# A hybrid trunk kernel on one core: kept weights reloaded in eight pieces, first write-backs postponed, and GLA score levels computed on half of the partitions

## The chip, the core and the metric

The kernel runs on one core of a Trainium2 chip. A core has a matrix engine (PE, with its weight loads shown as PEld), a vector engine (DVE), a scalar engine (ACT), GpSimd (POOL) and a sync engine (SP) whose instructions here only issue transfers; 16 DMA engines carry them. The metric is the device time of one execution in microseconds (us), lower is better.

## The reference

One layer of a trunk over 2048 tokens of width 1024. A single input projection feeds four groups of heads, each a causal recurrence, and one output projection merges them.

```python
u = rmsnorm(h, norm_w[l])
proj = (u @ w_in[l]).astype(f32)
...
y_a = gla_branch(a_q, a_k, a_v, a_gr, a_z, ...)
y_b = mlstm_branch(...)
y_c = hgrn2_branch(...)
y_d = ssd_branch(d_x, d_B, d_C, d_dt, d_z, ...)
mixed = jnp.concatenate([y_a, y_b, y_c, y_d], axis=-1)
h = h + mixed @ w_out[l]
```

GLA (gated linear attention, 4 heads with keys of width 64) scores a query i against each earlier key j of its chunk of 64 tokens with a decay of its own in each key dimension d:

```python
scores = jnp.einsum('bhid,bhjd,bhijd->bhij', qb, kb, decay)
out = (jnp.einsum('bhij,bhje->bhie', scores, vb)
       + jnp.einsum('bhid,bhde->bhie', qb * jnp.exp(G), state))
```

SSD (Mamba-2) works on chunks of 128 tokens: scores of C against B, masked by decays, applied to the inputs, plus a carried state.

## The kernel before, in words

**Halves and units.** The sequence is worked in two halves of 1024 tokens. In each, ten units follow each other: two of GLA (g0, g1, each a pair of heads, the first head's keys on partitions 0 to 63, the second's on 64 to 127), two of SSD (q0, q1), four of HGRN2 and two pairs of mLSTM. The output projection ends the program.

**Projections.** A unit takes its columns of the input projection in groups of 256 columns (`gqk0` holds queries and keys of g0, `gv0` values and gates, `gz0` the gating path, then g1's; for SSD `sx`, `sbc`, `sz`); there are 30 groups. In the first half a group's raw float32 weights of 1 MB are loaded (`raw`), ACT casts them to a coarse part `hi` (four casts, line 248), DVE computes the remainder `lo` (line 250), and a closure `keep` (line 236) writes both to DRAM as `wk`, called while a later group is loaded. In the second half hi and lo are loaded back from there (line 222). `hi` and `lo` have two buffers each, `raw` one. `weights(key)` hands out a group and starts the load of the next. With activations split the same way into uh and ul, each product is three matmuls (hi·uh, hi·ul, lo·uh) for each of 8 slices k of the 1024 inputs: `ps_c` (channels by 512 tokens), `ps_t` (128 tokens by 256 columns), and `ps_g` (128 tokens by 288, for `gv0`). All of them are issued on line 123, in `mm`.

**The start.** Rows of x (`o_f`, `o_qp`, ... `<-x`, line 169) are squared and summed on ACT (line 173), DVE turns the sums into a scale for each token (`ss`, lines 176 to 180), PE transposes it (`ps_rb`, line 188), and ACT scales the four waiting `ps_g` tiles with it into `o_v` (line 676).

**GLA scores.** `lin_unit` with `nh=2` goes through levels of block width b = 1, 2, 4, 8, 16, 32. At each, DVE multiplies decays into kb (line 516) and qf (line 517), PE multiplies keys by queries into `ps_s`, and DVE copies the entries that belong to the level into the score tiles `ST` under a mask (line 479 for b = 1, 4, 8, 16; lines 561 and 562 for b = 2). For b = 1, 4, 8, 16 a tile `qz` (shown as t2k) is built in which each head's queries stand on that head's partitions with zeros on the other's: POOL clears (line 491), ACT copies (line 492). There are four GLA units in all, so 16 such levels. An fp32 matmul appears as two instructions on PE.

**SSD.** A unit computes the conv inputs, then goes through 8 chunks. A step transposes with `ps_xt` (line 898), computes `ps_s` from `ct` (line 749), DVE forms the masked scores (line 911, from decays loaded as `ab<-rows`, line 884), and PE goes on with `ps_o` and `ps_u`. Between a step's `ps_s` and its `ps_o` stand projection matmuls of other units. Finished outputs go to DRAM as 64 KB stores `y<-t2k` (line 645).

**Order.** A scheduler fixes each engine's order of instructions at build time; an instruction waits for those ahead of it on its engine. All transfers named here are issued from SP in that order and use eight completion counters in turn, so each one waits for the one eight before it.

Of the kernel before, what the change touches and what calls it, by code (L numbers as in the profile page):

```python
# [10 lines left out]
F32 = mybir.dt.float32  # L11
# [10 lines left out]
P = 128  # L22
S = 2048
D = 1024
KT = D // P
TH = 1024
NH = S // TH
C = 128
NC = TH // C
# [87 lines left out]
class Kernel:  # L117
# [91 lines left out]
    def load_w(self, key, cuts=None):  # L209

        nc = self.nc
        gates = key == ("gv", 0)
        n = WG + (NG if gates else 0)
        hi = self.wp.tile([P, KT * (WG + NG)], F32R, tag="hi", name="hi", bufs=2)[:, :KT * n].rearrange("p (k n) -> p k n", k=KT)
        lo = self.wp.tile([P, KT * (WG + NG)], F32R, tag="lo", name="lo", bufs=2)[:, :KT * n].rearrange("p (k n) -> p k n", k=KT)
        self.wready[key] = hi, lo
        if self.ahead_of(key) > 0:
            for k in self.unwritten:
                k()
            self.unwritten = []  # L220
            for t, d in zip((hi, lo), self.wkept[key]):
                nc.sync.dma_start(t.bitcast(F32), d.bitcast(F32))
            return
        raw = self.wp.tile([P, KT * (WG + NG)], F32, tag="raw", name="raw")[:, :KT * n].rearrange("p (k n) -> p k n", k=KT)
        self.wkept[key] = [self.dram.tile([P, KT, n], F32R, tag=f"wk{GIDX[key]}{i}", name="wk") for i in range(2)]

        def part(k0, k1):
            nc.sync.dma_start(raw[:, k0:k1, :WG], self.a["w"][GIDX[key], :, k0:k1])
            if gates:
                nc.sync.dma_start(raw[:, k0:k1, WG:], self.a["wg"][:, k0:k1])  # L230
            nc.scalar.copy(hi[:, k0:k1], raw[:, k0:k1])
            nc.vector.tensor_tensor(lo[:, k0:k1], raw[:, k0:k1], hi[:, k0:k1].bitcast(F32), op=ALU.subtract)

        def keep():
            for d, t in zip(self.wkept[key], (hi, lo)):
                nc.sync.dma_start(d.bitcast(F32), t.bitcast(F32))


        kept, self.unwritten = self.unwritten, [keep]
        if cuts:  # L240
            return [(k0, lambda k0=k0, k1=k1: part(k0, k1)) for k0, k1 in zip(cuts, cuts[1:] + [KT])]
        nc.sync.dma_start(raw[:, :, :WG], self.a["w"][GIDX[key]])
        if gates:
            nc.sync.dma_start(raw[:, :, WG:], self.a["wg"])
        for k in kept:
            k()
        for k0, k1 in ((0, 2), (2, 4), (4, 6), (6, 8)):
            nc.scalar.copy(hi[:, k0:k1], raw[:, k0:k1])  # L248
        for k0, k1 in ((0, 4), (4, 8)):
            nc.vector.tensor_tensor(lo[:, k0:k1], raw[:, k0:k1], hi[:, k0:k1].bitcast(F32), op=ALU.subtract)  # L250
# [186 lines left out]
    def lin_unit(self, nh, f, kb, qp, v, sz, car, eps, ycol, vt=None):  # L437

        nc = self.nc
        rw = P // nh  # L440
        rows = [slice(h * rw, (h + 1) * rw) for h in range(nh)]
# [3 lines left out]
        STs = [self.next_st() for _ in range(nh)]  # L445
# [8 lines left out]
        def mixed(b, q):  # L454

            n = 64 // b
            mx = self.t2k().rearrange("p (c n two b) -> p c n two b", c=NC // 2, two=2, b=b)
            nc.scalar.copy(mx[:, :, :, 0], kb.rearrange("p (c u n two b) -> p c u n two b", c=NC // 2, u=2, two=2, b=b)[:, :, 0, :, 0])
            nc.scalar.copy(mx[:, :, :, 1], flipped(C - 1 - b, 2 * b, n, b))
            ps = self.psp.tile([P, NC // 2, 2, n, b], F32, tag="t", name="ps_s")  # L460
            for c in range(NC // 2):
                self.mm(ps[:, c], mx[:, c].rearrange("p n two b -> p (n two b)"), q[:, 2 * c:2 * c + 2])
            return ps
# [6 lines left out]
        def level(b, q, mo):  # L470

            m = mask[:, mo:mo + 64].rearrange("p (n b) -> p n b", b=b)[:, None]

            def place(h, c0, n, ps):
                if mo == 0:
                    o = STs[h][:, c0:c0 + n].rearrange("p c (n two b) -> p c n b two", two=2, b=1)[:, :, :, :, 0]
                else:
                    o = STs[h][:, c0:c0 + n].rearrange("p c (n two b) -> p c n two b", two=2, b=b)[:, :, :, 1]
                nc.vector.copy_predicated(o, m.to_broadcast([P, n, 64 // b, b]), ps)

            if nh == 1:
                ps = mixed(b, q)
                for t in range(2):
                    o = STs[0][:, t::2].rearrange("p c (n two b) -> p c n two b", two=2, b=b)[:, :, :, int(mo != 0)]
                    m = mask[:, 384 * t + mo:384 * t + mo + 64].rearrange("p (n b) -> p n b", b=b)[:, None]
                    nc.vector.copy_predicated(o, m.to_broadcast([P, NC // 2, 64 // b, b]), ps[:, :, t])
                return
            for g in range(2):
                qz = self.t2k().rearrange("p (c h n b) -> p c h n b", c=4, h=2, b=b)
                for h in range(2):  # L490
                    nc.gpsimd.memset(qz[rows[h], :, 1 - h], 0.0)
                    nc.scalar.copy(qz[rows[h], :, h], q[rows[h], 4 * g:4 * g + 4])
                ps = self.psp.tile([P, 4, 2, 64 // b, b], F32, tag="t", name="ps_s")
                for c in range(4):
                    cc = 4 * g + c
                    self.mm(ps[:, c].rearrange("p h n b -> p (h n b)"), kb[:, cc * C:(cc + 1) * C], qz[:, c].rearrange("p h n b -> p (h n b)"))
                for h in range(2):
                    place(h, 4 * g, 4, ps[:, :, h])

        level(1, qp[:, :, 0].unsqueeze(3), 0)  # L500
        if nh == 1:

# [7 lines left out]
        b = 1  # L510
        while b < C:
            n = TH // (2 * b)
# [14 lines left out]
            if b in (4, 8, 16):  # L527
                level(b, qf.rearrange("p (c n two b) -> p c n two b", c=NC, two=2, b=b)[:, :, :, 1], {4: 192, 8: 256, 16: 320}[b])
                continue
            if nh == 1:  # L530
                ST = STs[0]
                if b == 2:
                    kr = flip_odd()
                    for t in range(2):
                        ps = self.psp.tile([P, 4, 2, 64], F32, tag="t", name="ps_s")
                        for c in range(4):
                            cc = 2 * c + t
                            self.mm(ps[:, c].rearrange("p a b -> p (a b)"), kr[:, c] if t else kb[:, cc * C:(cc + 1) * C], qp[:, cc, 1:3].rearrange("p a b -> p (a b)"))
                        m = mask[:, 384 * t:384 * t + 384]
# [6 lines left out]
                ps = mixed(b, qf.rearrange("p (c n two b) -> p c n two b", c=NC, two=2, b=b)[:, :, :, 1])  # L546
# [5 lines left out]
            if b == 2:  # L552
                for g in range(2):
                    pss = [self.psp.tile([P, 4, 2, 64], F32, tag="t", name="ps_s") for _ in range(nh)]
                    for c in range(4):
                        cc = 4 * g + c
# [9 lines left out]
            elif b == 32:  # L566
                for r, ST in zip(rows, STs):
                    ps = self.psp.tile([P, NC, 32], F32, tag="t", name="ps_s")
# [5 lines left out]
            else:  # L574
                pss = [self.psp.tile([P, NC, 64], F32, tag="t", name="ps_s") for _ in range(nh)]
# [8 lines left out]
        for g in range(2):  # L584
            pt = self.psp.tile([P, 4, P], F32, tag="t", name="ps_kt")
            for c in range(4):
                cc = 4 * g + c
# [17 lines left out]
            for c in range(4):  # L605
                cc = 4 * g + c
# [563 lines left out]
```

## Time and profile before

| | before |
|---|---|
| median of 3 runs | 2164.32 us (2163.56 to 2164.61) |
| profiled execution | 2164.58 us, of which the span in the trace is 2162.8 us |
| mean granted PE clock | 0.988 of full |
| instructions | 34846 |

The span runs from the first to the last recorded instruction; what lies around it is 1.78 us. PE is the engine that is busy nearly all of the time, so the places where it is not are what to look for, and the chain of work that ended last says how long each link of it was.

### The profile page before, as it was taken

What the parts mean: (1) busy time and instruction counts of PE and PEld (TensorE: products, weight loads), DVE (VectorE), ACT (ScalarE), POOL (GpSimd) and SP (SyncE); (2) the same over time, 40 slices, a digit from 0 to 9 for tenths busy, and PEclk for the clock granted to TensorE, in tenths of its full rate; (3) what the DMA queues carried; (4) which work ended last, traced back from release to release, by engine and by line L of the source; (5) the groups of instructions that cost most, each with busy time, mean ns of one, the idle gap of its engine ahead of it and who ended that gap; (6) DMA issues with size and microseconds to landing.
All of it is one profiled execution on the core that took longest, in us unless ns stands there. A gap on an engine that the chain in (4) does not pass through costs nothing.

```text
span 2162.8 us, 34846 instructions
## 1 busy us (share of the span) xinstructions
PE 2101.6 (97%) x13758; PEld 1876.2 (87%) x13758; DVE 1211.3 (56%) x2892; ACT 773.0 (36%) x1947; POOL 81.7 (4%) x160
## 2 busy tenths in 40 slices
PE   7999999999999999999998999999999999999998
PEld 6988889998899999897987888898899998888887
DVE  4564868756676545626374956555654456533332
ACT  6632333444444344444221324333333334212111
POOL 0000011100000000000000111000000000000000
PEclk9999999999999999999998989999999999999999
DMA  8434344444244354521422233222232326422321
GB/s 309 151 109 128 92 152 137 147 138 128 78 121 147 127 176 152 164 101 45 134 62 95 82 104 109 72 68 90 77 119 69 127 90 194 142 97 89 107 73 49
DMA packets 197171, 251.41 MB, mean 116 GB/s; under 512 B 142344, under 2 KB 153720, under 8 KB 178064
## 3 DMA queue, kind: packets, MB, share of 16 engines
q1 hardware_dynamic: 190528, 229.79, 33.6%
q10 hardware_dynamic: 6480, 19.40, 2.6%
q8 instruction: 108, 1.77, 0.3%
q14 instruction: 55, 0.45, 0.1%
HBM read 160.70 MB, written 88.45 MB: 115 GB/s over the span
## 4 chain that ended last, share of the span: by engine, by line
PE 87%; DVE 5%; ACT 4%; DMA 3%; issue 1%; SPq 1%; POOL 0%; ACTq 0%; DVEq 0%
PE ps_t L123 31%; PE ps_c L123 24%; PE ps_out L123 15%; PE ps_o L123 6%; PE ps_s L123 5%; PE ps_u L123 3%; PE ps_g L123 2%; DMA ST<-w_out 1%; DMA t2k<-xT 1%; DVE kb L516 1%; DMA raw<-w 1%; PE ps_xt L898 1%; DVE ST L561 0%; ACT t2k L624 0%; DMA o_f<-x 0%
## 5 line engine op out<-in xcount | busy, mean ns | idle before, releaser
L123 PE MATMUL ps_t<-hi,uh 128*128 128x256 f32 x1920 | 545.0, 284 | 0.5 <-DVE craw L742 0.4
L123 PE MATMUL ps_t<-lo,uh 128*128 128x256 f32 x1920 | 545.5, 284 | 0.0
L123 PE MATMUL ps_t<-hi,ul 128*128 128x256 f32 x1920 | 545.4, 284 | 0.0
L123 PEld LDWEIGHTS ps_t<-hi,uh 128*128 128x128 f32 x1920 | 368.7, 192 | 2.3 <-DVE craw L742 1.0
L123 PEld LDWEIGHTS ps_t<-lo,uh 128*128 128x128 f32 x1920 | 369.2, 192 | 0.8
L123 PEld LDWEIGHTS ps_t<-hi,ul 128*128 128x128 f32 x1920 | 369.0, 192 | 0.5 <-issue 0.4
L123 PE MATMUL ps_c<-uh,hi 128*128 128x512 f32 x896 | 357.8, 400 | 7.3 <-ACT uh L155 7.3
L123 PE MATMUL ps_c<-ul,hi 128*128 128x512 f32 x896 | 355.9, 397 | 0.1
L123 PE MATMUL ps_c<-uh,lo 128*128 128x512 f32 x896 | 355.6, 397 | 0.0
L123 PEld LDWEIGHTS ps_c<-uh,hi 128*128 128x128 f32 x896 | 169.8, 190 | 40.1 <-ACT uh L155 7.7
L123 PEld LDWEIGHTS ps_c<-ul,hi 128*128 128x128 f32 x896 | 169.8, 189 | 33.8 <-DVE ul L156 1.0
L123 PEld LDWEIGHTS ps_c<-uh,lo 128*128 128x128 f32 x896 | 169.8, 190 | 33.5
L301 ACT ACTIVATE v<-ps_t,ss 128x128 f32<-128x128 f32 x128 | 40.3, 362 | 168.0 <-PE ps_t L123 167.9
L980 DVE TENSOR_TENSOR o_sz<-o_sz,ps_out 128x512 f32<-128x512 f32 (+1 forms) x33 | 22.1, 671 | 129.9 <-PE ps_out L123 127.6
L123 PE MATMUL ps_out<-woh,o_qp 128*128 128x512 f32 x288 | 94.2, 395 | 0.0
L296 ACT ACTIVATE sz<-ps_t,ss 128x128 f32<-128x128 f32 (+1 forms) x160 | 54.2, 387 | 102.4 <-PE ps_t L123 95.2
L297 DVE SCALAR_TENSOR_TENSOR sz<-sz,ps_t 128x256 f32<-128x256 f32 (+1 forms) x80 | 37.8, 473 | 80.0 <-ACT sz L296 79.7
L250 DVE TENSOR_TENSOR lo<-raw,hi 128x1024 fp32r<-128x1024 f32 (+1 forms) x58 | 70.7, 1227 | 16.6 <-ACT hi L248 16.2
L248 ACT CAST hi<-raw 128x512 fp32r<-128x512 f32 (+1 forms) x116 | 66.1, 626 | 30.5 <-PE ps_c L123 21.2
L123 PE MATMUL ps_out<-woh,o_v 128*128 128x512 f32 (+1 forms) x213 | 75.4, 389 | 0.0
L784 DVE TENSOR_TENSOR t2k<-t2k,ps_s 128x512 f32<-128x512 f32 x16 | 11.0, 688 | 103.2 <-PE ps_s L123 99.1
L123 PEld LDWEIGHTS ps_out<-woh,o_qp 128*128 128x128 f32 x288 | 54.1, 188 | 12.9
(362 smaller groups left out, 3620.3 us busy)
## 6 DMA issues: line engine op xcount, KB each, us to landing
raw<-w SPq DMA_DIRECT2D x29, 1024.0 KB, 6.7
wk<-hi SPq DMA_DIRECT2D x29, 1024.0 KB, 8.2
wk<-lo SPq DMA_DIRECT2D x29, 1024.0 KB, 9.7
lo<-wk SPq DMA_DIRECT2D x29, 1024.0 KB, 6.8
hi<-wk SPq DMA_DIRECT2D x29, 1024.0 KB, 6.0
y<-t2k SPq DMA_DIRECT2D x256, 64.0 KB, 2.0
t2k<-y SPq DMA_DIRECT2D x64, 256.0 KB, 3.7
t2k<-xT SPq DMA_DIRECT2D x32, 256.0 KB, 4.3
```

The lines of the kernel that those rows point to most:

```text
L123: self.nc.tensor.matmul(out, l, r, start=start, stop=stop, skip_group_check=shared)
L248: nc.scalar.copy(hi[:, k0:k1], raw[:, k0:k1])
L250: nc.vector.tensor_tensor(lo[:, k0:k1], raw[:, k0:k1], hi[:, k0:k1].bitcast(F32), op=ALU.subtract)
L296: nc.scalar.activation(out[:, j], ps[:, j], AF.Tanh, scale=self.rsh[:, t + j:t + j + 1])
L297: nc.vector.scalar_tensor_tensor(out=out, in0=out, scalar=1.0, in1=ps, op0=ALU.add, op1=ALU.mult)
L301: self.nc.scalar.activation(out[:, j], ps[:, j], AF.Identity, scale=sc[:, t + j:t + j + 1])
L516: nc.vector.tensor_tensor(kv[:, :, 0], kv[:, :, 0], pv[:, :, 1:2].to_broadcast([P, n, b]), op=ALU.mult)
L784: nc.vector.tensor_tensor(dt, dt, ps, op=ALU.mult)
L898: nc.tensor.transpose(pt[:, i * P:(i + 1) * P], src[:, cs], self.ident)
L980: nc.vector.tensor_tensor(xt[:, ns], xt[:, ns], ps, op=ALU.add)
```

## The change

Three edits are made at once. In `load_w`, the second half's reload of a group is issued as eight transfers (four pairs of slices k, hi and lo of each in turn, 256 KB each, 288 KB for `gv0`) where there were two of 1 MB. Also in `load_w`, the first write-backs come later: nothing is written at the second group, only the first group's parts at the third, and both the second's and the third's at the fourth; from there on each group's are written at the next, as before. The third group's casts go into the first group's buffer. In `lin_unit` with two heads, the levels b = 1, 4, 8, 16 no longer build `qz`: keys and queries of one head are multiplied on that head's 64 partitions, 16 matmuls of 64 partitions by 64 columns for 8 of 128 by 128, with no clearing and no copies, into one tile for each head, and one masked copy for each head takes the place of two.

```diff
@@ load_w, the second half's reload
-            for t, d in zip((hi, lo), self.wkept[key]):
-                nc.sync.dma_start(t.bitcast(F32), d.bitcast(F32))
+            for k in range(0, KT, 2):
+                for t, d in zip((hi, lo), self.wkept[key]):
+                    nc.sync.dma_start(t[:, k:k + 2].bitcast(F32), d[:, k:k + 2].bitcast(F32))
             return
...
-        kept, self.unwritten = self.unwritten, [keep]
+        n = len(self.wkept)
+        kept = self.unwritten[:1] if n == 3 else [] if n == 2 else self.unwritten
+        self.unwritten = self.unwritten[len(kept):] + [keep]
...
@@ lin_unit, level
-            for g in range(2):
-                qz = self.t2k().rearrange("p (c h n b) -> p c h n b", c=4, h=2, b=b)
-                for h in range(2):
-                    nc.gpsimd.memset(qz[rows[h], :, 1 - h], 0.0)
-                    nc.scalar.copy(qz[rows[h], :, h], q[rows[h], 4 * g:4 * g + 4])
-                ps = self.psp.tile([P, 4, 2, 64 // b, b], F32, tag="t", name="ps_s")
-                for c in range(4):
-                    cc = 4 * g + c
-                    self.mm(ps[:, c].rearrange("p h n b -> p (h n b)"), kb[:, cc * C:(cc + 1) * C], qz[:, c].rearrange("p h n b -> p (h n b)"))
-                for h in range(2):
-                    place(h, 4 * g, 4, ps[:, :, h])
+            pss = [self.psp.tile([P, NC, 64 // b, b], F32, tag="t", name="ps_s") for _ in range(nh)]
+            for c in range(NC):
+                for r, ps in zip(rows, pss):
+                    self.mm(ps[:, c], kb[r, c * C:(c + 1) * C], q[r, c])
+            for ST, ps in zip(STs, pss):
...
+                nc.vector.copy_predicated(o, m.to_broadcast([P, NC, 64 // b, b]), ps)
```

The new order of the engines shows the edits at four engines and in places where the code was not touched.

**The start, SP.** SP's queue right behind the load of `gv0`'s raw weights, before; `wk<-hi` of 128x2048 is the first group's write-back.

```order
L236 DMA wk<-hi 128x2048
L236 DMA wk<-lo 128x2048
L169 DMA o_f<-x 128x1024 x2
L169 DMA o_qp<-x 128x1024
L169 DMA o_kb<-x 128x1024
L169 DMA o_f<-x 128x1024 x2
L169 DMA o_qf<-x 128x1024
L169 DMA o_pl<-x 128x1024
L242 DMA raw<-w 128x2048
```

The same place in the changed kernel:

```order
L169 DMA o_f<-x 128x1024 x2
L169 DMA o_qp<-x 128x1024
L169 DMA o_kb<-x 128x1024
L169 DMA o_f<-x 128x1024 x2
L169 DMA o_qf<-x 128x1024
L169 DMA o_pl<-x 128x1024
L246 DMA raw<-w 128x2048
L237 DMA wk<-hi 128x2048
L237 DMA wk<-lo 128x2048
```

The eight loads of x rows and the raw load of `gz0` now stand ahead of the first group's write-backs.

**The start, ACT.** ACT's queue at the end of the squares (line 173), before; line 248 casts `gz0`'s weights, line 676 scales `ps_g`.

```order
L173 ACTIVATE o_pl,ss<-o_pl 128x1024
L248 CAST hi<-raw 128x512 x4
L676 ACTIVATE o_v<-ps_g,ss 128x256 x4
L190 COPY t2k<-ps_rb 8x128
L676 ACTIVATE o_v<-ps_g,ss 128x256 x3
```

The same place in the changed kernel, where the casts are line 252 and the scaling is line 672:

```order
L173 ACTIVATE o_pl,ss<-o_pl 128x1024
L672 ACTIVATE o_v<-ps_g,ss 128x256 x4
L190 COPY t2k<-ps_rb 8x128
L252 CAST hi<-raw 128x512 x4
L672 ACTIVATE o_v<-ps_g,ss 128x256 x4
```

The scaling of the four waiting `ps_g` tiles has moved ahead of the casts.

**SSD's q0 in the second half, PE.** PE's queue where the first step begins, before; `ps_t` is the projection of the gating path `sz0`, `ps_xt`, `ps_s` and `ps_o` are the step's.

```order
L123 MATMUL ps_c<-uh,lo 128x512
L123 MATMUL ps_t<-hi,uh 128x256 x3
L898 MATMUL ps_xt<-cf,xc 128x128 x2
L898 MATMUL ps_xt<-cf,v 128x128
L123 MATMUL ps_t<-hi,uh 128x256
L123 MATMUL ps_s<-ct,v 128x128
L123 MATMUL ps_o<-t2k 128x64 x4
L123 MATMUL ps_o<-hst,ct 128x256
L123 MATMUL ps_t<-lo,uh 128x256
```

The same step in the changed kernel:

```order
L123 MATMUL ps_t<-lo,uh 128x256
L123 MATMUL ps_t<-hi,ul 128x256
L894 MATMUL ps_xt<-cf,xc 128x128 x2
L894 MATMUL ps_xt<-cf,v 128x128
L123 MATMUL ps_s<-ct,v 128x128
L123 MATMUL ps_c<-uh,hi 128x512
```

All 192 matmuls of `ps_t` now stand ahead of the step's `ps_xt`, where four stood before it or between its parts, and projection matmuls `ps_c` stand between `ps_s` and `ps_o`.

In the second SSD unit of that half, the second step looks like this on PE before, between two transposes:

```order
L898 MATMUL ps_xt<-cf,v 128x128
L123 MATMUL ps_s<-ct,v 128x128
L123 MATMUL ps_c<-uh,lo 128x512
L123 MATMUL ps_o<-t2k 128x64 x4
L123 MATMUL ps_o<-hst,ct 128x256
L123 MATMUL ps_u<-t2k 128x256
L898 MATMUL ps_xt<-cf,xc 128x128 x2
L898 MATMUL ps_xt<-cf,v 128x128
```

Of projection matmuls, the first three steps there have, by the order, 8, 1 and 18 between `ps_s` and `ps_o` before, and 19, 19 and 19 in the changed kernel.

**A GLA level, DVE.** DVE's queue in g0 of the first half from level b = 4 on, before; `ST_93` and `ST_95` are the score tiles of the two heads.

```order
L479 COPY_PREDICATED ST_93<-mask,ps_s 128x64x4
L479 COPY_PREDICATED ST_95<-mask,ps_s 128x64x4
L517 TENSOR_TENSOR qf<-qf,pl 128x32x16
L479 COPY_PREDICATED ST_93<-mask,ps_s 128x64x4
L479 COPY_PREDICATED ST_95<-mask,ps_s 128x64x4
L516 TENSOR_TENSOR kb<-kb,pl 128x128x4
```

The same place in the changed kernel:

```order
L494 COPY_PREDICATED ST_93<-mask,ps_s 128x128x4
L494 COPY_PREDICATED ST_95<-mask,ps_s 128x128x4
L512 TENSOR_TENSOR kb<-kb,pl 128x128x4
L513 TENSOR_TENSOR qf<-qf,pl 128x128x4
L494 COPY_PREDICATED ST_93<-mask,ps_s 128x64x8
L494 COPY_PREDICATED ST_95<-mask,ps_s 128x64x8
```

Two masked copies of double width (line 494) take the place of four, and the multiplication of qf (now line 513) stands behind the level's copies and ahead of the next level, no longer between the copies.

## Rows read from the trace of the kernel before

**Rows 1.** The page: busy time by engine; the chain by engine.

```profile
PE 2101.6 (97%) x13758; PEld 1876.2 (87%) x13758; DVE 1211.3 (56%) x2892; ACT 773.0 (36%) x1947; POOL 81.7 (4%) x160
...
PE 87%; DVE 5%; ACT 4%; DMA 3%; issue 1%; SPq 1%; POOL 0%; ACTq 0%; DVEq 0%
```

**Rows 2.** Timeline of the start, by engine: start, duration, instruction [idle before <-releaser].

```profile
23.55 2.61 SPq L236 DMA_DIRECT2D wk<-hi  x1
...
26.68 2.25 SPq L169 DMA_DIRECT2D o_f<-x  x2
...
35.82 1.06 ACT L173 ACTIVATE o_f<-o_f 128x1024 f32<-128x1024 f32 x1 [2.35 <-DMA o_f<-x]
...
50.55 2.18 ACT L248 CAST hi<-raw 128x512 fp32r<-128x512 f32 x4 [2.76 <-DMA raw<-w]
...
47.82 0.17 DVE L176 TENSOR_SCALAR ss<-ss 128x8 f32<-128x8 f32 x1 [14.26 <-ACT o_pl L173]
...
50.52 0.37 PE L188 MATMUL ps_rb<-cf,ss 128*8 128x128 f32 x1 [5.24 <-issue]
...
53.15 0.61 PE L123 MATMUL ps_g<-hi,uh 128*128 128x288 f32 x1 [2.26 <-ACT o_v L676]
```

**Rows 3.** Timeline of the second half's first projections: SP's queue, then PE.

```profile
897.83 0.42 SPq L222 DMA_DIRECT2D hi<-wk  x1
...
916.11 0.49 SPq L222 DMA_DIRECT2D lo<-wk  x1
...
922.26 0.40 PE L123 MATMUL ps_g<-lo,uh 128*128 128x288 f32 x1 [2.14 <-DMA lo<-wk]
```

**Rows 4.** Timeline of the second half's SSD units: SP's queue, then PE.

```profile
1132.07 0.43 SPq L222 DMA_DIRECT2D lo<-wk  x1
...
1150.59 0.77 PE L123 MATMUL ps_s<-ct,v 128*128 128x128 f32 x2 [7.37 <-DVE ct L749]
...
1152.20 1.97 PE L123 MATMUL ps_o<-t2k 128*128 128x64 f32 x8 [0.85 <-DVE t2k L911]
...
1268.06 1.96 PE L123 MATMUL ps_o<-t2k 128*128 128x64 f32 x8 [2.03 <-DVE t2k L911]
...
1276.47 1.97 PE L123 MATMUL ps_o<-t2k 128*128 128x64 f32 x8 [3.14 <-DVE t2k L911]
```

**Rows 5.** Windows: those stretches, and first half's q0; length, busy (x), clock, DMA.

```profile
1142.00:1165.00 23.00, 14.68 (x90) 13.80 (x89) 10.24 (x19) 3.49 (x6) 1.52 (x2) 0.70 0.24 92
...
1263.00:1311.00 48.00, 42.09 (x204) 34.77 (x203) 27.94 (x75) 14.12 (x28) 7.55 (x10) 0.86 0.26 77
...
285.00:330.00 45.00, 44.98 (x240) 37.86 (x239) 40.02 (x88) 16.17 (x35) 7.65 (x10) 1.00 0.41 128
```

**Rows 6.** Timeline of GLA's levels and an SSD step; one chain piece.

```profile
106.82 2.06 PE L123 MATMUL ps_s<-qp,kb 64*128 64x128 f32 x32 [0.59 <-DVE kb L516]
...
119.10 1.95 PE L123 MATMUL ps_s<-t2k,kb 128*128 128x128 f32 x16
...
1299.88 1.07 PE L123 MATMUL ps_o<-t2k 128*128 128x64 f32 x8 [0.41 <-DVE t2k L911]
...
104.85 1.31 DVE L479 COPY_PREDICATED ST<-mask,ps_s 128x256 f32<-128x256 uint8 x2
...
120.19 1.66 DVE L479 COPY_PREDICATED ST<-mask,ps_s 128x256 f32<-128x256 uint8 x4 [2.66 <-PE ps_s L123]
...
121.75 0.69 DVE L516 TENSOR_TENSOR kb<-kb,pl 128x512 f32<-128x512 f32 x1
...
1231.63 8.87 PE ps_c L123 x39
```

**Rows 7.** The page, DMA issues: count, KB each, us from issue to landing.

```profile
hi<-wk SPq DMA_DIRECT2D x29, 1024.0 KB, 6.0
...
t2k<-xT SPq DMA_DIRECT2D x32, 256.0 KB, 4.3
...
ab<-rows SPq DMA_DIRECT2D x16, 512.0 KB, 5.0
```

More of the change, by code (lines that the diff above doesn't have):

```diff
@@ L472, in level @@
             m = mask[:, mo:mo + 64].rearrange("p (n b) -> p n b", b=b)[:, None]
[L474 to L479, printed above, removed]
             if nh == 1:
@@ L487, in level @@
                 return
-            for g in range(2):
-                qz = self.t2k().rearrange("p (c h n b) -> p c h n b", c=4, h=2, b=b)
-                for h in range(2):
-                    nc.gpsimd.memset(qz[rows[h], :, 1 - h], 0.0)
-                    nc.scalar.copy(qz[rows[h], :, h], q[rows[h], 4 * g:4 * g + 4])
-                ps = self.psp.tile([P, 4, 2, 64 // b, b], F32, tag="t", name="ps_s")
-                for c in range(4):
-                    cc = 4 * g + c
-                    self.mm(ps[:, c].rearrange("p h n b -> p (h n b)"), kb[:, cc * C:(cc + 1) * C], qz[:, c].rearrange("p h n b -> p (h n b)"))
-                for h in range(2):
-                    place(h, 4 * g, 4, ps[:, :, h])
+            pss = [self.psp.tile([P, NC, 64 // b, b], F32, tag="t", name="ps_s") for _ in range(nh)]
[3 more added lines that the diff above has]
+            for ST, ps in zip(STs, pss):
+                if mo == 0:
+                    o = ST.rearrange("p c (n two b) -> p c n b two", two=2, b=1)[:, :, :, :, 0]
+                else:
+                    o = ST.rearrange("p c (n two b) -> p c n two b", two=2, b=b)[:, :, :, 1]
+                nc.vector.copy_predicated(o, m.to_broadcast([P, NC, 64 // b, b]), ps)
         level(1, qp[:, :, 0].unsqueeze(3), 0)
```

## The prediction

> **What bounds the kernel now.** I read four views, in this order. The page first: PE is busy for 2101.6 of 2162.8 us, and 87% of the chain that ended last is PE [rows 1]. So the program is as long as PE's work plus the places where PE stands still or runs at a lower clock; the sum of PE's idle time is 2162.8 − 2101.6, about 61 us. A change that takes no matmuls out can gain only from those places. The timeline of PE, read for its idle times alone, then shows where they are, and the largest that I found are few: 5.24 and 2.26 us at the start [rows 2], 2.14 us at the second half's first `ps_g` [rows 3], and 7.37, 0.85, 2.03 and 3.14 us in the SSD units of the second half [rows 4], 23 us together. Third, the timelines of SP, ACT and DVE at the same moments say what was late. Last, the windows give the granted clock there: 0.70 and 0.86 around the SSD gaps against 1.00 in the same stage of the first half [rows 5].
>
> The profiled execution took 2164.58 us, 1.78 us more than its span and 0.26 us above the median of the three runs. I make the sum against 2164.6.
>
> **The first write-backs, moved later.** Nothing of it adds or removes a byte. Before, the write-backs of the first group are issued at 23.55 us and the x rows behind them at 26.68 us, so the rows lose 26.68 − 23.55 = 3.1 us by the order of the queue alone. The first row reaches ACT only at 35.82, 9.1 us after its issue [rows 2], where the same 512 KB land in 5.0 us elsewhere [rows 7]: some 4 us more go by sharing the DMA engines with 2 MB that nobody waits for. The squares end at 47.8, the scale is ready at 50.5, PE waits 5.24 us for it, then ACT casts `gz0`'s weights for 2.18 us before it scales the first `ps_g`, and PE waits another 2.26 us [rows 2]. After the change the rows are issued first, and ACT scales ahead of the casts. Squares that begin 3 to 7 us earlier cover 5.24 us of wait, and the order on ACT covers the 2.26. Bounds: 3.1 us (the issue time alone comes back) and 7.5 us (both gaps close). I take 6, nearer the upper one, because two separate delays go. What is late next is the cast of `gz0`, which now also waits for the write-back of the first group; PE has the other four tokens of `gv0` to work on meanwhile. If that cover fell short, the gap would be what the write takes beyond it, a few us at most.
>
> **The reload in eight pieces, at `gv0` of the second half.** Before, hi is issued at 897.83 us and lo only at 916.11, behind eight stores of y, and PE waits 2.14 us for lo at 922.26 [rows 3]. After, hi and lo of the first two slices both go ahead of those stores, and PE's order works through four tokens on these slices before it needs the next. That wait goes; with the half-clock stretch behind it I take 2.5 us (bounds 0, if the later pieces are waited for instead, and 3.5).
>
> **The same, in the SSD units.** Here the order changes most. Before, lo of `sz0` is issued at 1132.07 us, behind sixteen stores of y, and the first SSD step stands ahead of `sz0`'s projection: PE waits 7.37 us for `ct` and 0.85 for the masked scores [rows 4]. After, the 192 `ps_t` come first, as in the first half, whose window of that stage shows PE busy for 44.98 of 45 us at clock 1.00 [rows 5]. In the second unit the steps get 19 projection matmuls each where they had 8, 1 and 18; a matmul takes 8.87/39 = 0.227 us, so 19 take 4.3 us [rows 6], while the wait behind 8 matmuls is 2.03 us and behind one 3.14 [rows 4]. 8 matmuls, 1.8 us, left 2.03 us of wait, so some 4 us are needed and 19 suffice. The gaps are worth 7.37 + 0.85 + 2.03 + 3.14 = 13.4 us. To that comes the clock. In 1142 to 1165, PE is idle for 8.3 us and the granted clock is 0.70, which is 13.8 us at 1.2 GHz and the rest at 2.4 GHz; 5.5 us of work was done at half speed and would have taken half of that, a loss of 2.8 us. In 1263 to 1311 (0.86: 13.4 us at 1.2 GHz, 5.9 idle) 7.5 us of work at half speed, 3.8 lost. Together 13.4 + 2.8 + 3.8 = 20 us. I take all of it, since the first half shows the new order without a gap (bounds 0, if the waits only move, and 20).
>
> What the pieces cost: 8 issues of 0.42 to 0.49 us [rows 3, 4] for 2, some 2.7 us more of SP's time for each of 30 groups. SP's issue time lies beside PE's; it costs only where something urgent stands behind the pieces (third rival). A sentence by itself: the Trainium skill ("DMA: Bandwidth & Descriptors", Bandwidth) asks for at least 1 MiB in a DMA if most of the peak rate is wanted. The trace agrees in kind, with 6.0 us for 1024 KB against 4.3 for 256 KB [rows 7], but bandwidth is not what PE waits for here, so it adds nothing to the sum.
>
> **GLA's levels on half arrays.** There are 16 such levels. Each loses, by the code, 4 clears on POOL and 4 copies on ACT, which are busy for 4% and 36% [rows 1] and work while PE does other matmuls; I cost their removal at nothing. PE: the level before is 16 instructions in 1.95 us. The nearest row to the new one is level b = 2, which already runs on 64 partitions, 32 instructions with 128 columns in 2.06 us [rows 6]. Whether 64 columns make it shorter is not shown directly. `ps_o` with 64 columns and a weight of 128 takes 1.07 us for 8 instructions, 0.134 for each, and the old level, with 128 columns, 1.95/16 = 0.122 [rows 6]. Halving the columns against a full-width weight does not pay there. So I take 2.06: +0.11 × 16 = +1.8 us. If it did halve, 1.03, it would be −0.92 × 16 = −14.7 us.
>
> The wait behind it: DVE's copies took 1.66 us for four at b ≥ 8, but the first two ran beside PE's second half of the level. After, two of double width (at most the same 1.66) start when the level ends, then kb at 0.69, then qf at about the same, which can't run earlier since PE reads qf in place. That is a chain of 3.0 us, where the fillers are 12 matmuls or 12 × 0.227 = 2.7 us [rows 6]. Three steps in each of four units: 12 × 0.3 = 3.6 us of new waits (bounds 0, and 8 if each of 16 levels waits 0.5). Together +1.8 + 3.6 = +5.4 us; bounds −14.7 and +9.8.
>
> **Sum.** 2164.6 − 6 − 2.5 − 20 + 5.4 = 2141.5, say 2141 us. All bounds at once would be 2118.9 and 2171.3.
>
> **The rivals.**
> 1. *The half arrays pay* (0.10). The b = 2 row speaks against it only if its length comes from weights and not from its 128 columns; it fits both. Then each level is 1.03 us, the fillers no longer cover DVE's chain, and the 3.6 us of waits stay: −14.7 + 3.6 = −11.1 in place of +5.4, 2164.6 − 28.5 − 11.1 = 2125 us. The Trainium skill ("TensorEngine Tiling (Array Packing)", Theoretical Speedup) has this rule, up to twice the speed where a dimension is at most 64; by the rows of b = 2 and `ps_o` no more than the two heads side by side comes of it, which only makes up for the doubled number of instructions.
> 2. *The SSD gaps come back elsewhere* (0.14). Fillers that now stand in q0 and q1 are taken from some later stage, and PE waits there as it did here. For it: PE is 97% busy and the matmuls are the same. Against: the first half runs that order without a gap [rows 5]. With none of the 20 left, 2161.5 us, with half 2151.5.
> 3. *SP's queue gets in the way* (0.07), the case of slower. In SP's order an `ab` load can stand behind eight pieces. They take some 2.7 us more to issue, and as each transfer waits for the one eight before it, the load can be held until the first piece has landed, 4.3 us [rows 7]. An SSD step needs its `ab` before `ps_o`. Half of the 16 `ab` loads, 8, lie in the second half; if each came 4 us too late, 2141 + 32 = 2173 us. It decides once each is more than some 2.9 us late beyond its cover. Against it: the load is issued ahead of its step, with two 4.3 us steps of fillers to hide in.
>
> **How the numbers follow.** The forecast holds 0.69. 0.2% is 4.3 us, about what a measurement of this kernel can tell from no change, so faster means below 2160, slower above 2168.7. The forecast and the first rival are faster (0.79), half of the second too (0.07); the other half is no change (0.07); the third is slower (0.07). The range 2122 to 2157 takes in the first rival and the half-way case of the second; it leaves out the third (0.07), the full second (0.07) and some 0.05 at the ends.
>
> **What would show it.** Right: the PE waits at 50 us under 1.5 us together; none above 1 us at the second half's first `ps_g` lo; q0's first `ps_s` in the second half without a wait, and both windows near clock 1.00; `ps_s` on 64 partitions with 64 columns at about 2.06 us for 32 instructions, with waits of 0.3 us for qf behind some. Wrong: levels near 1.0 us (first rival), a new PE wait of some us in HGRN2 or later, or a wait for an `ab` transfer at `ps_o`. The prediction stands or falls with the 20 us of SSD.

## The result and the profile after

The changed kernel takes 2137.94 us (median of 4 runs, 2137.24 to 2143.25) where the kernel before takes 2163.94: a ratio of 0.9889, 95% interval 0.9878 to 0.9901. The forecast was 2141 us, in the range 2122 to 2157. The profiled execution took 2138.02 us, 26.56 us less than the one of before.

The page after: the span, the busy times and the chain by engine.

```profile
span 2136.2 us, 35274 instructions
...
PE 2095.6 (98%) x14014; PEld 1869.4 (88%) x14014; DVE 1206.0 (56%) x2860; ACT 750.8 (35%) x1885; POOL 62.1 (3%) x96
...
PE 88%; DVE 5%; ACT 3%; DMA 3%; issue 1%; SPq 0%; POOL 0%; ACTq 0%; DVEq 0%; POOLq 0%
```

PE is busy for 6 us less than before, and its idle time falls from about 61 to 41 us by the page [rows 1]. Apart from the GLA levels the matmuls on PE are the same, so the gain is in waits and in the clock, as the prediction said.

The start after, as start, duration and instruction for SP, ACT and PE:

```profile
24.75 3.31 SPq L169 DMA_DIRECT2D o_f<-x  x2
...
37.92 0.60 SPq L237 DMA_DIRECT2D wk<-hi  x1
...
33.05 1.05 ACT L173 ACTIVATE o_f<-o_f 128x1024 f32<-128x1024 f32 x1
...
48.08 1.57 ACT L672 ACTIVATE o_v<-ps_g,ss 128x256 f32<-128x256 f32 x4 [3.02 <-DVE o_state L671]
...
50.38 2.19 ACT L252 CAST hi<-raw 128x512 fp32r<-128x512 f32 x4 [0.62 <-DMA wk<-hi]
...
47.79 0.27 PE L188 MATMUL ps_rb<-cf,ss 128*8 128x128 f32 x1
...
48.61 0.40 PE L123 MATMUL ps_g<-hi,uh 128*128 128x288 f32 x1 [0.55 <-ACT o_v L672]
```

The first x rows are issued at 24.75 us and the first write-back only at 37.92. The first square is at 33.05 (35.82 before), and PE's waits of 5.24 and 2.26 us [rows 2] are down to one of 0.55. The ACT scaling now precedes the casts, and the cast of `gz0`'s weights waits for the write-back of the first group, but only 0.62 us.

The second half after: SP's queue at `gv0` and at `sz0`, then PE at the SSD units.

```profile
906.24 0.42 SPq L223 DMA_DIRECT2D lo<-wk  x1
...
907.80 4.36 SPq L641 DMA_DIRECT2D y<-t2k  x8
...
1116.46 0.32 SPq L223 DMA_DIRECT2D hi<-wk  x1
...
1120.44 0.32 SPq L223 DMA_DIRECT2D lo<-wk  x1
...
1127.11 9.56 SPq L641 DMA_DIRECT2D y<-t2k  x16
...
1161.61 0.39 PE L123 MATMUL ps_s<-ct,v 128*128 128x128 f32 x2
...
1166.16 1.00 PE L123 MATMUL ps_o<-t2k 128*128 128x64 f32 x8
...
1259.44 1.10 PE L123 MATMUL ps_o<-t2k 128*128 128x64 f32 x8 [0.36 <-DVE t2k L907]
...
1267.43 1.08 PE L123 MATMUL ps_o<-t2k 128*128 128x64 f32 x8 [1.05 <-DVE t2k L907]
```

At `gv0` the first piece of lo goes at 906.24, ahead of the stores. At `sz0` all eight pieces have gone by 1120.44, and the sixteen stores follow at 1127.11. The first SSD step's `ps_s` at 1161.61 and `ps_o` at 1166.16 carry no wait; before they waited 7.37 and 0.85 us [rows 4]. In q1 a wait of 0.36 and one of 1.05 are left of 2.03 and 3.14.

The windows of those two stages after (length, busy of PE, PEld, DVE, ACT, POOL, clock, DMA share, GB/s):

```profile
1142.00:1165.00 23.00, 23.00 (x182) 22.47 (x181) 8.18 (x15) 5.00 (x11) 0.00 (x0) 1.00 0.30 91
...
1247.00:1295.00 48.00, 46.30 (x279) 40.36 (x279) 32.75 (x89) 18.99 (x36) 8.62 (x12) 1.00 0.40 121
```

PE is busy for all of 23 us and for 46.3 of 48, at a granted clock of 1.00, where the clock was 0.70 and 0.86 [rows 5]. The first window now ends ahead of the step's `ps_o`, because the step comes later; PE has no wait above 0.15 us from the end of GLA to q1's 0.36.

The GLA levels b = 4, 8 and 16 of g0 after, on PE and on DVE:

```profile
109.65 2.00 PE L123 MATMUL ps_s<-qf,kb 64*128 64x64 f32 x32 [1.87 <-DVE kb L512]
...
116.13 2.00 PE L123 MATMUL ps_s<-qf,kb 64*128 64x64 f32 x32
...
118.06 0.51 PE L123 MATMUL ps_c<-uh,lo 128*128 128x512 f32 x1
...
121.00 2.00 PE L123 MATMUL ps_s<-qf,kb 64*128 64x64 f32 x32
...
118.16 1.31 DVE L494 COPY_PREDICATED ST<-mask,ps_s 128x512 f32<-128x512 uint8 x2 [4.01 <-PE ps_s L123]
...
119.37 0.68 DVE L512 TENSOR_TENSOR kb<-kb,pl 128x512 f32<-128x512 f32 x1
...
119.97 0.69 DVE L513 TENSOR_TENSOR qf<-qf,pl 128x512 f32<-128x512 f32 x1
```

A level takes 2.00 us for 32 instructions, near the forecast 2.06. The two copies take 1.31 us, then kb and qf follow, and the next level at 121.00 has no wait.

### The profile page after: what moved, and what is told of

Same layout as the page of the kernel before. It is cut to its first block, busy times and chain, and to the rows that moved or that the text cites. A ratio compares the mean times of both kernels' runs of the same rounds, so it can differ in the third digit from the quotient of the medians.

```text
span 2136.2 us, 35274 instructions
## 1 busy us (share of the span) xinstructions
PE 2095.6 (98%) x14014; PEld 1869.4 (88%) x14014; DVE 1206.0 (56%) x2860; ACT 750.8 (35%) x1885; POOL 62.1 (3%) x96
## 4 chain that ended last, share of the span: by engine, by line
PE 88%; DVE 5%; ACT 3%; DMA 3%; issue 1%; SPq 0%; POOL 0%; ACTq 0%; DVEq 0%; POOLq 0%
PE ps_t L123 30%; PE ps_c L123 25%; PE ps_out L123 15%; PE ps_o L123 6%; PE ps_s L123 5%; PE ps_u L123 3%; PE ps_g L123 2%; DMA ST<-w_out 1%; DMA t2k<-xT 1%; DVE kb L512 1%; DMA hi<-wk 1%; DVE ST L494 0%; ACT t2k L620 0%; DVE ST L557 0%; PE ps_xt L894 0%
## 5 line engine op out<-in xcount | busy, mean ns | idle before, releaser
L301 DVE SCALAR_TENSOR_TENSOR sz<-sz,ps_t 128x256 f32<-128x256 f32 (+1 forms) x80 | 37.5, 471 | 70.6 <-ACT sz L300 70.2
L123 PEld LDWEIGHTS ps_out<-woh,o_qp 128*128 128x128 f32 x288 | 54.1, 188 | 13.7 <-ACT woh L936 0.9
```

Of the source, the lines that this page charges most:

```text
L123: self.nc.tensor.matmul(out, l, r, start=start, stop=stop, skip_group_check=shared)
L301: nc.vector.scalar_tensor_tensor(out=out, in0=out, scalar=1.0, in1=ps, op0=ALU.add, op1=ALU.mult)
```

## The time by stretches of equal work

By the order of instructions, PE has done the same projection matmuls in every kernel at the first SSD transpose `ps_xt` of the first half, at the first `ps_xt` of q1 in the second half, and at the first mLSTM scores of the second half. Where GLA ends in the second half (its last `ps_kt` group), kernels with half arrays have already done 13 more `ps_c`; 13 × 0.227 = 2.9 us are taken off for that, so the second and third stretch there are worked out and not read. All times in us, from each profiled execution.

| stretch | before | changed | pieces alone | later writes alone | half arrays alone | pieces and later writes | half arrays and later writes |
|---|---|---|---|---|---|---|---|
| start, GLA of the first half | 284.9 | 281.9 | 283.0 | 277.7 | 288.8 | 279.2 | 280.8 |
| to the end of GLA, second half | 817.1 | 816.6 | 814.7 | 815.5 | 822.1 | 811.2 | 821.8 |
| to q1 (this is q0) | 161.4 | 148.8 | 157.6 | 161.1 | 148.9 | 156.7 | 148.9 |
| q1 and HGRN2 | 319.5 | 308.9 | 310.9 | 318.5 | 310.7 | 308.3 | 310.7 |
| the rest | 579.9 | 580.0 | 578.7 | 580.1 | 579.6 | 578.4 | 580.2 |
| median of the runs | 2163.9 | 2137.9 | 2144.4 | 2157.9 | 2151.7 | 2136.4 | 2144.7 |

The table is read by columns against "before" for one edit alone, and by pairs for one edit on top of others: the pieces on top of the two others are "changed" against the last column, the half arrays on top are "changed" against "pieces and later writes".

One trace of each kernel stands behind these rows, and a trace scatters. The pieces act in the second half alone, yet "before" and "pieces alone" differ by 1.9 us in the first row. From the second row on the later writes have no edit left, yet "pieces alone" and "pieces and later writes", whose order on PE is the same there, differ by 3.5 us in the second row and 2.6 in the fourth. In the row of q0 such pairs lie within 1 us. So a difference of 2 or 3 us outside q0 is not shown by one pair of columns.

## The experiments

Medians of several rounds beside runs of the kernel before, whose median was 2163.6, 2163.0 and 2163.0 us in the three groups. The ratios are against those runs, with their 95% intervals.

**The pieces alone.**

```diff
-            for t, d in zip((hi, lo), self.wkept[key]):
-                nc.sync.dma_start(t.bitcast(F32), d.bitcast(F32))
+            for k in range(0, KT, 2):
+                for t, d in zip((hi, lo), self.wkept[key]):
+                    nc.sync.dma_start(t[:, k:k + 2].bitcast(F32), d[:, k:k + 2].bitcast(F32))
```

> The kernel before with only the reload in eight pieces. Theory 1 (the prediction: the pieces let the second half's SSD units keep their projection matmuls, and give gv0 its lo in time): 20 us from SSD and 2.5 to 5.8 us from gv0, so 2138 to 2142 us, with the start's two PE waits (5.24 and 2.26 us) and the GLA levels as before. Theory 2 (the SSD gain is the order that the scheduler makes, and any edit may bring it, the GLA edit too): the same time here, since this order has 164 and then 19 to 22 fillers in the SSD steps; the two part in c_only. Rival (the pieces cost SP's queue more than they give): above 2160 us, with waits for ab or y transfers.

Measured: 2144.4 us (ratio 0.9912, 0.9898 to 0.9925). It falls short, and the table shows where: q1 gains 8.6 us, q0 only 3.8. SP's queue at `sz0`, and PE at q0's first step:

```profile
1116.73 0.42 SPq L223 DMA_DIRECT2D hi<-wk  x1
...
1118.30 9.43 SPq L646 DMA_DIRECT2D y<-t2k  x16
...
1127.77 0.50 SPq L223 DMA_DIRECT2D lo<-wk  x1
...
1146.14 0.77 PE L123 MATMUL ps_s<-ct,v 128*128 128x128 f32 x2 [4.62 <-DVE ct L750]
```

Only three pieces are issued ahead of the sixteen stores, and the other five stand behind them, from 1127.77. The order has 28 of the `ps_t` ahead of the step, where all 192 stand ahead in the changed kernel, and PE still waits 4.62 us for `ct`. The pieces alone do not do what the prediction credited them with in q0.

**The later write-backs alone.**

```diff
-        kept, self.unwritten = self.unwritten, [keep]
+        n = len(self.wkept)
+        kept = self.unwritten[:1] if n == 3 else [] if n == 2 else self.unwritten
+        self.unwritten = self.unwritten[len(kept):] + [keep]
```

> The kernel before with only the later first write-backs. Both theories: the PE waits at 50 us close, about 5 us less (the changed kernel was 5.2 us ahead at the same point of the work), so 2159 us, and the SSD units keep their waits of 7.4, 2.0 and 3.1 us, as the order of their steps is that of before (0 fillers in q0's first step, 8, 1 and 18 in q1's). Rival (the write-backs moved later collide with gz0's cast): 2162 us or more, with a PE wait at gz0's projection.

Measured: 2157.9 us (0.9970, 0.9959 to 0.9980). PE behind the scale, and at q0's first step in the second half:

```profile
48.43 0.40 PE L123 MATMUL ps_g<-hi,uh 128*128 128x288 f32 x1 [0.55 <-ACT o_v L678]
...
1141.86 0.77 PE L123 MATMUL ps_s<-ct,v 128*128 128x128 f32 x2 [7.37 <-DVE ct L751]
```

The start's waits are gone but for 0.55, and the first stretch is 7.2 us shorter. q0's wait is as before to the hundredth, 7.37 us.

**The half arrays alone.** This is the edit of `level` in the diff above, and nothing else.

> The kernel before with only the GLA levels on half arrays, no pieces and no later writes. Theory 1 (the SSD gain comes from the pieces): only the levels' cost is left, 2169 to 2172 us. Theory 2 (it comes from the order, which this edit changes by itself to 19 fillers in each early SSD step of the second half): 2163.9 - 20 + 5 to 8 = 2149 to 2152 us, with the wait for lo of gv0 and the start's waits as before. If the order has the fillers but the transfers come too late for them: about 2160 us, with PE waiting for lo<-wk of sz0.

Measured: 2151.7 us (0.9944, 0.9931 to 0.9956). Theory 1 is refuted: without a single piece, the SSD stage gains 12.5 us in q0 and 8.8 in q1, while GLA costs 3.9 and 5.0 us in the first two stretches. SP's queue at `sz0`:

```profile
1128.93 0.32 SPq L222 DMA_DIRECT2D hi<-wk  x1
...
1129.36 0.37 SPq L222 DMA_DIRECT2D lo<-wk  x1
...
1139.57 9.61 SPq L638 DMA_DIRECT2D y<-t2k  x16
```

Both whole reloads of 1 MB go ahead of the stores, which come 10 us later. With 13 more filler matmuls used up inside GLA, the order of everything behind it has moved, and the reload is in front of the stores instead of behind. That the one brings about the other is read from the two orders; it was not tested by itself.

**The pieces and the later write-backs, levels as before.** The first two diffs together.

> The pieces and the later write-backs, with GLA's levels as before. Both theories: the changed kernel without what the half arrays cost, by marks at equal work in the two traces +2.1 us in the first half and +5.5 us in the second, so 2137.9 - 7.6 = 2130 us. Rival (the half arrays give back elsewhere, by the freed ACT and POOL or by the order of SSD): 2138 us or more, slower than the changed kernel.

Measured: 2136.4 us (0.9876, 0.9862 to 0.9889), not 2130. The levels' cost is gone (2.7 and 5.4 us in the first two stretches), but q0 has its wait of 4.62 us for `ct` again and is 7.9 us longer. So the half arrays cost 8.1 us in GLA and give 7.9 us back in q0 by the order alone; the two kernels can't be told apart by their intervals.

**The half arrays and the later write-backs, whole reloads.** The changed kernel without the first diff.

> The changed kernel without the pieces: later first write-backs and half arrays, two reloads of 1 MB for each group. If the order brings the SSD gain and the pieces only feed gv0: the run with the half arrays alone (2151.7 us) less the start (7.2 us at the first SSD transpose), 2144.5 us, some 6 us above the changed kernel, and all of that 6 us before the second half's GLA levels. If the pieces also carry part of the SSD gain here: 2150 us or more, with waits in the SSD units.

Measured: 2144.7 us (0.9915, 0.9902 to 0.9929), as the first case said. What the pieces add on top is 5.2 us in the second stretch and 1.8 in the fourth; PE at `gv0` without them:

```profile
916.67 0.40 PE L123 MATMUL ps_g<-lo,uh 128*128 128x288 f32 x1 [0.79 <-DMA lo<-wk]
```

That wait is only 0.79 us, so the 5.2 us are more than this one wait. Most of them lie in the clock of the GLA levels: over this stretch the granted clock is 0.50 for 17.1 us in the trace without the pieces (13.7 of them in g0, from 978 to 999 us) and for 10.2 us in that of the changed kernel, and PE is busy all of that time, so the difference is worth 3.4 us. That the pieces are what changes the clock there is not shown.

**The stores of y on POOL's queue.** The kernel before with this one line, and none of the three edits:

```diff
-            nc.sync.dma_start(self.y[t0:t0 + 4, ...
+            nc.gpsimd.dma_start(self.y[t0:t0 + 4, ...
```

> The kernel before with one edit that is not in the change: the stores of y are issued from POOL's queue, so that no reload stands behind them on SP; loads whole, levels and write-backs as before. If the stores ahead of lo on SP are the cause of the SSD waits (the order then has 19 fillers or more in every early step, and 192 ps_t ahead of q0's first step): 2163.9 - 23 - 2 to 5 for gv0 = 2136 to 2139 us, with the start's waits of 7.5 us kept. If the stores are not the cause, the waits for ct and for the masked scores stay and it is 2160 us or more; the same if 128 stores cost POOL so much that its clears for the GLA levels come late.

Measured: 2134.3 us (0.9863, 0.9848 to 0.9878). This one line gives at least as much as the three edits together. SP's queue at `sz0` and PE behind the scale, then the stores by count, size and time to landing:

```profile
1113.56 0.32 SPq L222 DMA_DIRECT2D hi<-wk  x1
...
1113.97 0.38 SPq L222 DMA_DIRECT2D lo<-wk  x1
...
48.59 0.37 PE L188 MATMUL ps_rb<-cf,ss 128*8 128x128 f32 x1 [4.40 <-issue]
```

```profile
y<-t2k POOLq DMA_DIRECT2D x256, 64.0 KB, 2.6
```

hi and lo are issued one behind the other, 0.41 us apart (1120.09 and 1132.07 us before). q0 takes 149.1 us and q1 with HGRN2 308.1, as in the changed kernel, with whole reloads. The start keeps a wait of 4.40 us. The stores land in 2.6 us instead of 2.0, and no PE wait is put down to them.

**The stores on ACT's queue.** The same line with `nc.scalar`.

> As the one on POOL, but with the stores on ACT's queue. Same cause, same gain in the second half (2136 to 2141 us); a rival is that ACT, which also casts and scales in its order, waits for the stores' data, and PE for ACT: then SSD's waits go but new ones behind ACT come, 2145 us or more.

Measured: 2150.2 us (0.9941, 0.9928 to 0.9953), the rival's case. q0 has lost its wait here too, but PE waits elsewhere, in SSD and HGRN2 of the first half:

```profile
328.99 1.10 PE L123 MATMUL ps_o<-t2k 128*128 128x64 f32 x8 [2.10 <-DVE t2k L911]
...
490.22 1.16 PE L123 MATMUL ps_s<-qf,t2k 128*128 128x128 f32 x8 [2.09 <-ACT t2k L459]
...
493.44 2.04 PE L123 MATMUL ps_s<-qf,t2k 128*128 128x128 f32 x8 [2.06 <-DVE qf L517]
```

The stores stand in ACT's order and wait there for DVE's transposes, and PE waits for what ACT and DVE do behind them: across the eight stores at 464.68 us ACT stands idle for 10.26 us. Where the stores go matters as much as that they leave SP.

**GLA levels cut by blocks of 64 tokens too.** On top of the changed kernel:

```diff
-                for r, ps in zip(rows, pss):
-                    self.mm(ps[:, c], kb[r, c * C:(c + 1) * C], q[r, c])
+                for u in range(2):
+                    for r, ps in zip(rows, pss):
+                        self.mm(ps[64 * u:64 * u + 64, c], kb[r, c * C + 64 * u:c * C + 64 * u + 64], q[r, c, u * nb:(u + 1) * nb])
...
+                for u in range(2):
+                    h, n = slice(64 * u, 64 * u + 64), slice(u * nb, (u + 1) * nb)
+                    nc.vector.copy_predicated(o[h, :, n], m[h, :, n].to_broadcast([64, NC, nb, b]), ps[h])
```

> The changed kernel with each GLA level cut once more, by blocks of 64 tokens: 32 matmuls of 64 partitions by 64 weight columns by 32 columns for 16 of 64 by 128 by 64, into the same scores, and four masked copies on 64 partitions for two on 128. If the level's time is the weight columns that pass (the rows of the changed kernel: 32 instructions take 2.00 us with weights of 128 columns and 1.15 with 64) and the four blocks lie side by side: 64 instructions in 1.1 to 1.2 us, 16 x 0.85 = 13.6 us less on PE, less some 4 us of waits for DVE's copies, so 2128 us. If the blocks of one head follow each other, 2.3 us a level and 2142 to 2146 us.

Measured: 2123.1 us (0.9814, 0.9800 to 0.9827). A level on PE, and its copies on DVE:

```profile
114.71 1.14 PE L123 MATMUL ps_s<-qf,kb 64*64 64x32 f32 x64
...
115.90 1.81 DVE L498 COPY_PREDICATED ST<-mask,ps_s 64x256 f32<-64x256 uint8 x4 [2.75 <-PE ps_s L123]
```

64 instructions with weights of 64 columns take 1.14 us where 32 with weights of 128 columns take 2.00, so the four blocks do lie side by side. DVE's four copies take 1.81 us for 1.31, two waits of about 0.5 us for qf appear, and the four waits for kb ahead of b = 2 are 1.14 to 1.23 us where the changed kernel has 0.80 to 0.91. That is the price, and it is small: up to the end of GLA, PE is idle for 32.2 us where the changed kernel has 29.3. The time is 5 us under the 2128 expected.

**Both together, with and without the pieces.** The last kernel with the stores on POOL, and the same with whole reloads.

> The changed kernel with the quartered GLA levels and the stores of y on POOL's queue. If the stores on SP were what delayed the reloads, and the order already avoids that in the run with the quartered levels, nothing is left for this to gain: 2121 to 2124 us. A gain above 2 us would say that some reload still came late behind stores.

> The same without the pieces: two reloads of 1 MB for each group, quartered levels, later first write-backs, stores on POOL. If the pieces only made up for the stores ahead of the reloads, they are worth nothing once the stores are gone: within 2 us of its twin with the pieces (2121 to 2124 us). If the finer transfers have a worth of their own (the first slices land earlier), 3 to 6 us above it, with a PE wait for lo<-wk at gv0 of the second half.

Measured: 2121.9 us with the pieces (0.9812, 0.9795 to 0.9829) and 2122.1 without (0.9805, 0.9792 to 0.9819). Once no store stands ahead of a reload, eight pieces and two whole reloads are the same, here in kernels with quartered levels. Neither is told apart from the 2123.1 us of the quartered levels. These three beat both kernels of the study, by some 15 us and 41 us.

## Why the prediction was right, and where it was not

**The start** was forecast at 6 us. Alone it gave 7.2 in its stretch, some of which may be scatter, and 5.7 in the medians; PE's idle time in the first stretch falls from 23.0 to 17.4 us. Both steps of the argument show: the rows go first, and ACT scales ahead of the casts. What was given back is ahead of that: in the changed kernel PE waits 1.56 us at 31.47 for hi of `gv0` and 1.56 at 33.44 for its lo, where before it was 1.23 us at 32.35. The casts of that group start 1.1 us later (30.75 for 29.66), of which 0.65 is there already when the last part of its load is issued (23.14 for 22.49), ahead of the rows. The rows now go out right behind that load; that they share the DMA engines with it is a likely reason for the other 0.4, not one that was tested.

**`gv0`** was forecast at 2.5 us. lo now goes ahead of the stores, as argued, and the wait of 2.14 us for it is gone, with one of 0.47 us ahead of it. So the term has about the right size at its place. The pieces gave 2.4 us in the second stretch alone, 4.3 on top of the later writes, and 5.2 on top of both others; what goes beyond 2.6 lies within the scatter of the traces or, in the last pair, in the clock of the GLA levels. The half-clock stretch behind the wait (923.35 to 926.76 us) is in the trace of before, but not in that of the later writes alone, which has the same wait at 1.85 us.

**SSD** was forecast at 20 us and measured 12.6 + 10.6 = 23.2. The waits that went are those that were named, with the clock going to 1.00. Of the named 13.4 us, 1.4 are left in q1, so 19 matmuls do not quite suffice there, and smaller waits of 1.5 us went with them. The term that was mis-sized is the clock. The sum took all of PE's idle time in the two windows, 8.3 and 5.9 us, as spent at half clock (1.2 GHz). The windows of the two stretches at half clock, with columns as above, show that only 6.2 and 3.1 us of them are idle, and the rest is work:

```profile
1145.22:1158.87 13.65, 7.44 (x31) 6.99 (x32) 6.41 (x12) 1.57 (x2) 0.79 (x1) 0.50 0.23 98
...
1268.10:1281.75 13.65, 10.51 (x37) 8.97 (x38) 6.46 (x19) 0.89 (x2) 2.79 (x4) 0.50 0.34 101
```

PE works for 7.44 and 10.51 us at half clock before, and not at all in q0 and q1 after. That is a loss of 3.7 + 5.3 = 9.0 us where the sum had 2.8 + 3.8 = 6.6. The step that failed is "the same, in the SSD units": the gain was put down to the pieces, because the order showed the new place of `ps_t`, and the pieces were the edit on the reload. The half arrays alone bring 21.3 us of it, the pieces alone 12.4. What they have in common is that lo of `sz0` gets out of the way of sixteen stores; moving the stores to another queue does it too, with whole reloads. Over all the kernels it holds: where all of that reload is issued ahead of the stores, or the stores are not on SP, the order has all 192 `ps_t` ahead of the step's `ps_s` and PE has no wait; where only three pieces go ahead, 28 and a wait of 4.62 us; where only hi does, 4 and a wait of 7.37. PE's wait itself is for DVE's `ct` and not for lo, so a late lo acts through the order that is fixed at build time; no run kept the order and moved only the transfer. The order of the three edits together showed that a wait would go; it did not show which edit moved it. Building the order of each edit alone would have shown that the half arrays by themselves put 19 fillers into the early steps.

**GLA** was forecast at +5.4 us and cost 8.1 on top of the others, 8.9 alone. Both its terms were off, and a third was left out. First what follows the level b = 8 on PE before; then windows, up to the end of GLA in the second half and of the levels of its g1, each for the changed kernel and then for the pieces and later write-backs:

```profile
120.80 0.48 PE L123 MATMUL ps_c<-ul,hi 128*128 128x512 f32 x1
...
0.00:1101.38 1101.38, 1072.07 (x7895) 970.95 (x7895) 663.86 (x1500) 436.10 (x1077) 34.91 (x58) 0.99 0.43 134
...
0.00:1090.30 1090.30, 1062.71 (x7626) 966.22 (x7626) 663.87 (x1530) 461.01 (x1141) 54.51 (x122) 0.99 0.43 136
...
1065.00:1100.00 35.00, 32.15 (x326) 26.11 (x326) 22.37 (x34) 4.38 (x10) 0.00 (x0) 0.90 0.19 61
...
1054.00:1089.00 35.00, 32.48 (x312) 28.52 (x311) 20.60 (x40) 7.83 (x18) 1.83 (x6) 1.00 0.19 61
```

The levels: the instruction rows, 1.95 and 2.00 us, understate the difference, because PE's rows overlap. From the start of a level to the start of what follows it is 120.80 − 119.10 = 1.70 us before and 118.06 − 116.13 = 1.93 after, so 0.23 and not 0.11. Not every level is at that price (four of those before that ran at full clock took 1.78 or 1.81), so 16 levels are at most 3.7 us. The waits: those for qf, 3.6 us in the sum, are not there in the levels shown, since two copies of double width take 1.31 us and not 1.66, and 12 fillers cover the chain. In their place the four waits for kb ahead of b = 2 are each some 0.3 to 0.6 us longer. All in all PE is idle for 29.3 us up to the end of GLA and for 27.6 without the half arrays, 1.7 us more. The clock was not in this sum at all. In g1 of the second half it is 0.90 over 35 us against 1.00: PE runs at half clock from 1077.83 to 1084.65, without a gap, and loses 3.4 us. The three add up: 1.7 + 3.4 leaves 3.0 of the 8.1 us for the levels. The clock term is that of these two traces; in the kernel before there is a half-clock stretch of 3.4 us in the same unit. In the half arrays alone it is larger: 37.5 us at half clock up to the end of GLA against 20.5 before, which is most of the 8.9 us.

**The rivals.** The half arrays do not pay by halving the columns: 2.00 us against 2.06 at b = 2, which has twice the columns. The Trainium skill's rule ("TensorEngine Tiling (Array Packing)", Theoretical Speedup) speaks of more where both dimensions are small; the quartered level agrees in kind, 1.14 us against 2.00 for the same scores. SP's queue did not get in the way: no PE wait is put down to an `ab` load. Little came back elsewhere: 1.28 us at the first `ps_out` (0.46 and 0.82) where it was 0.17.

The forecast came within 3.1 us. By the stretches, SSD gave 3.2 us more than its term, 2.4 of it in the clock. The start, `gv0` and GLA together gave 3.5 us where their terms came to 3.1, and that is in part luck: GLA cost 2.7 us more than forecast, and the stretches of the other two gave about as much more than theirs.

## What to carry to other kernels

When several edits change a static order, build the order of each edit alone before a gain is put down to one of them: here three different edits (the half arrays, and the stores on POOL's or on ACT's queue) each closed the same wait. A load that feeds the bound engine should not share an in-order queue with many stores that wait for a late engine: before, SP's queue stands still for 245.1 us in all for DVE ahead of the stores of y, and at `sz0` sixteen of them take 9.5 us to issue. One line that moved them gave as much as three edits. Here a step on half of the array paid only once the weights got narrower too. Read the price of a step from start to next start, not from the row's duration, and count the clock behind a wait with the wait.

## What the runs showed that was not expected

The time of these fp32 score levels goes with the columns of the weights: 32 instructions with weights of 64 by 128 take 2.06 us with 128 moving columns and 2.00 with 64, and with weights of 64 by 64 and 64 moving columns, the step behind b = 32, 1.15. In the quartered level 64 instructions with weights of 64 by 64 and 32 moving columns take 1.14. At b = 32, 64 instructions with weights of 64 by 32 take 1.11, but there the two heads are issued one after the other; whether weights below 64 columns bring more is open.

The largest waits of PE in GLA were not in the prediction's list and are still there. Ahead of the level b = 4 of each GLA unit PE waits 2.05 to 2.86 us before and 1.87 to 2.70 after. In seven of these eight cases the granted clock falls to 0.50 within 2.3 us of the end of the wait and stays there for 3.4 us or, once, 6.8.

A masked copy on 64 partitions costs as much as on 128: four of 64x256 take 1.81 us, four of 128x256 took 1.66 [rows 6].

POOL's queue takes 64 KB stores at 0.65 us each to issue, and they land in 2.6 us, with no PE wait put down to them.
